# A hybrid encoder layer on one core: first loads of weight sums on POOL's queue, an own sum buffer in the last block, and separate columns for the final norm

## The chip, the core and the metric

The kernel runs on one core of one Trainium2 chip. The metric is the device time in microseconds. The engines are named as in the profile: PE is TensorE (PEld its weight loads), DVE VectorE, ACT ScalarE, POOL GpSimd, and SP SyncE, which here only issues transfers. Each of SP, ACT and POOL has a queue of transfers of its own; in the profile's queue names q1 is SP's, q10 ACT's and q0 POOL's ("software").

## The reference, cut to what matters

```python
x += 1/2 * SwiGLU_1(RMSNorm(x))          # 1024 -> 2816 -> 1024, 512 tokens
x += concat(ssd_out, attn_out) @ W_out   # a mixer between the two
x += 1/2 * SwiGLU_2(RMSNorm(x))
return rms_norm(x, final_norm)

def swiglu(h, w_gate, w_up, w_down):
    return (jax.nn.silu(h @ w_gate) * (h @ w_up)) @ w_down
```

All is float32. What follows touches the two feed-forward layers (FFN1, FFN2) and the final norm; the mixer is not changed.

## The kernel before

**Three matmuls for one.** Each float32 operand is split into a high part (a cast on ACT) and a low part (a subtraction on DVE); a product is then three matmuls. For a unit of weights the cast is line 272 and the subtraction line 274 (`usplit`); the results go to four pairs of `xw` tiles in turn.

**Units.** The 22 tiles of the hidden dimension are taken in 11 pairs, d = 0 to 10. In FFN1 d = 0 and 1, in FFN2 d = 0 are computed plainly in four units, A11, A21, A12, A22 (gate and up, each over half of the inner dimension: A12 and A22 need the second half of `x`). All others are computed with seven products of sums, P1 to P7, as in Strassen's scheme, and so are the down projections, in blocks of up to four d's; a piece c of a block is two d's. In the names below A[0] to A[3] are the four quarters of the weights of one d, W0 to W3 those of a piece of the down projection ("a0", "a10": its first d). A unit's weights are 512 KB in SBUF as 128 x 1024 floats; the last piece, a10, has half of that.

**Sums made by transfers.** P5 needs A[2]+A[3]; P6 adds A[0] to that, P3 adds A[1]. The sum stands in one of four half-buffers in the wide tiles s40 and s52: `first` (line 324) copies A[2] into it from SP's queue, `more` (line 327) adds the others by accumulating transfers, which only POOL issues. P7 adds a quarter onto the raw tile `g` of P1, also through POOL. Plain quarters are loaded raw by SP into four `raw` buffers (line 320).

**Order.** `program` lists the units in the order in which PE takes them. Weights are split three units ahead of their use (`Stream.get`), and each job's transfers are issued some units ahead, as its list of moves says (`(14, before, first)`: at most 14 units ahead and, once the job `before` has been split, which is when its buffer comes free). A scheduling layer sets the order on each engine from this.

**The last block.** The down projection of FFN2's last three d's (8, 9, 10) runs as ("S", 2, P, pieces): its first units take one piece at a time. P6 and P3 of piece a10 take the buffer in which P5's sum stood.

**The final norm.** `after2` runs when a 128-token tile t of one half o of `x` is complete: Square with a sum on ACT, a multiplication by the norm's weights on DVE, and, when both halves of a tile are there, the columns v, sqrt, reciprocal and one Newton step (`rq_*` tags, one buffer each), then the scalings and the transfers out.

Of the kernel before, what the change touches and what calls it, by code (L numbers as in the profile page):

```python
# [14 lines left out]
P = 128  # L15
# [22 lines left out]
def hybrid_block(ctx: ExitStack, tc, xT, xt, par, wgu1, wd1, ws1, win, wdt, wv, wo, rbt, wgu2, ws2, fin, out):  # L38
# [50 lines left out]
    class Job:  # L89
# [6 lines left out]
        def move(self, ahead, force=False):  # L96
            while self.moves and (force or ahead <= self.moves[0][0]):
                lead, after, fn = self.moves[0]
                if after == "raw":

                    after = ws.raws[-4] if len(ws.raws) > 3 else None
                    if not after or after.parts is not None:
                        ws.raws.append(self.holds)
                if after and after.parts is None:
                    assert not force
                    return
                fn()
                self.moves.pop(0)
# [172 lines left out]
    def program(plain, by_tokens):  # L281


        if plain == 1:
            out = [("A11", 0), ("A21", 0), ("A12", 0), ("P1", 1), ("P5", 1), ("A22", 0), ("P6", 1), ("P2", 1), ("P7", 1)]
        else:
            out = [(a, d) for d in range(plain) for a in ("A11", "A21", "A12", "A22")]
            out += [(p, plain) for p in ("P5", "P1", "P6", "P2", "P7")]
        out = [("P", p, d) for p, d in out]
        for d in range(plain + 1, ND):  # L290
            out += [("P", p, e) for p, e in (("P5", d), ("P1", d), ("P3", d - 1), ("P4", d - 1), ("P6", d), ("P2", d),
                                             ("P7", d))]
            for n in range(2):
                if d == BLOCKS[n][1]:
                    out += [("S", n, p, (0, 1)) for p in DOWN]
        last = [("P", p, ND - 1) for p in ("P3", "P4")]
        if by_tokens == 3:
            return out + last + [("S", 2, p, (c,)) for c in range(2) for p in ("P5", "P1") + ("P2",) * (c == 0)] + [
                ("S", 2, "P6", (0, 1)), ("S", 2, "P2", (1,))] + [("S", 2, p, (0, 1)) for p in ("P7", "P3", "P4")]
        out += [("D", 2, 0, 0)] + last + [("D", 2, 1, 0), ("D", 2, 0, 1), ("D", 2, 1, 1)]  # L300
        return out + [("D", 2, o, c) for o in range(2, KD) for c in range(2)]

    def ffn_weights(wgu, plain, by_tokens, wst, wd=None):


        bufs, jobs, views = {}, {}, []

        def view(d):
            if d not in bufs:
# [11 lines left out]
            return go  # L321

        def first(d, src):
            return lambda: nc.sync.dma_start(out=view(d), in_=src)

        def more(get, src):
            return lambda: G.dma_start(out=get(), in_=src, accum_op=ALU.add)  # L327
# [1 line left out]
        def product(p, d, A):  # L329

            sum_ = lambda: view(d)
            raw = {"P1": "g", "P2": "g2", "P4": "u2"}.get(p)
            if p[0] == "A":
                n = ("A11", "A12", "A21", "A22").index(p)
                j = Job(lambda: usplit(bufs[p, d]), (6, "raw", whole((p, d), A[n])))
            elif raw:
                j = Job(lambda: usplit(bufs[raw, d]), (6 if p == "P1" else 5, "raw",
                                                       whole((raw, d), A[("P1", "P2", "", "P4").index(p)])))
            elif p == "P5":
                views.append(d)  # L340
                before = jobs["P3", views[-5]] if len(views) > 4 else None
                j = Job(lambda: usplit(view(d)), (14, before, first(d, A[2])), (10, None, more(sum_, A[3])))
            elif p == "P6":
                j = Job(lambda: usplit(view(d)), (6, jobs["P5", d], more(sum_, A[0])))
            elif p == "P7":
                j = Job(lambda: usplit(bufs["g", d]), (6, jobs["P1", d], more(lambda: bufs["g", d], A[2])))
            else:
                j = Job(lambda: usplit(view(d)), (6, jobs["P6", d], more(sum_, A[1])))
            jobs[p, d] = j
            if p == "P7":  # L350
                jobs["P1", d].holds = j
            ws.jobs.append(j)
# [20 lines left out]
    class XCombos:  # L373
# [13 lines left out]
        def col(self, k):  # L387
            return pt[:, self.wcol + k:self.wcol + k + 1]
# [53 lines left out]
    def ffn(xc, n_plain, early, by_tokens, rc, between, after):  # L442
# [174 lines left out]
        for step in program(n_plain, by_tokens):  # L617
            if step[0] == "S":
                while later:
                    later.pop(0)()  # L620
                if step[1:3] == (2, "P6"):
                    next(between, None)
                down(*step[1:])
                past = step[1:3] == (1, DOWN[-1])
                continue
# [680 lines left out]
    fw = []  # L1306
    ssq = sb("rcol", [P, 2, NC])

    def after2(o, t):

        if (o, t) == (0, 0):

            S.activation(out=sb("rq_o0", [P, 1]), in_=ones[:, 0:1], func=AF.Sqrt)
        v = x[:, 4 * o:4 * o + 4, t * P:(t + 1) * P]
        sq = sb("fh", [P, SEQ], bufs=2)
        four = lambda t: t.rearrange("p (a b) -> p a b", a=4)
        S.activation(out=four(sq), in_=v, func=AF.Square, accum_out=ssq[:, o, t:t + 1])
        y[o, t] = slot(4 + 2 * t + o, None, F32)
        V.tensor_tensor(out=four(y[o, t]), in0=v, in1=four(fw[o]), op=ALU.mult)
        if o == t // 2 or t == 2:  # L1320
            return
        n = slice(2, 4) if t == 3 else slice(t, t + 1)
        N = [P, n.stop - n.start]
        v0 = sb("rq_o1", N)
        V.tensor_scalar(out=v0, in0=ssq[:, 1 - o, n], scalar1=1.0 / D, scalar2=EPS, op0=ALU.mult, op1=ALU.add)
        v = sb("rq_v", N)
        V.scalar_tensor_tensor(out=v, in0=ssq[:, o, n], scalar=1.0 / D, in1=v0, op0=ALU.mult, op1=ALU.add)
        sd = sb("rq_q", N)
        S.activation(out=sd, in_=v, func=AF.Sqrt)
        i = sb("rq_y", N)  # L1330
        V.reciprocal(out=i, in_=sd)
        q = sb("rq_t", N)
        V.tensor_tensor(out=q, in0=i, in1=i, op=ALU.mult)
        r = sb("rq_r", N)
        V.scalar_tensor_tensor(out=r, in0=q, scalar=-0.5, in1=v, op0=ALU.mult, op1=ALU.mult)
        rs = sb("rq_o0", N)
        V.scalar_tensor_tensor(out=rs, in0=r, scalar=1.5, in1=i, op0=ALU.add, op1=ALU.mult)
        for t in range(n.start, n.stop):
            for h in range(2):
                c = rs[:, t - n.start:t - n.start + 1]  # L1340
                if h == 0 or t > 1:
                    S.activation(out=y[h, t], in_=y[h, t], func=AF.Copy, scale=c)
                else:
                    V.tensor_scalar(out=y[h, t], in0=y[h, t], scalar1=c, scalar2=None, op0=ALU.mult)
                (nc.sync if h else S).dma_start(out=out[:, t, h * SEQ:(h + 1) * SEQ], in_=y[h, t])

    y = {}
    ffn(xc3, 1, early2, 3, rc, between2(), after2)


# [61 lines left out]
```

## Time and profile before

| what | value |
|---|---|
| runs | 1039.98, 1036.24, 1032.68 us; median 1036.24 us |
| profiled execution | 1034.42 us, span 1032.6 us |
| PE busy | 1007.5 us, 98% of the span |
| DVE, ACT, POOL busy | 809.0, 587.9, 162.2 us |
| mean granted TensorE clock | 0.995 |
| POOL's queue | 59.78 MB, 33.2% of the 16 DMA engines' span |
| SP's queue | 95.43 MB, 27.3% |

PE is busy nearly throughout, so the time before can only be shortened where PE waits, ahead of its first or behind its last matmul; it can be lengthened wherever something that PE needs comes later.

### The profile page before, as it was taken

How to read it: one execution, taken by the hardware profiler on the slowest of the kernel's cores; microseconds unless marked ns; L12 is line 12 of the kernel's file. 1: busy time of each engine (PE TensorE's matmuls, PEld its weight loads, DVE VectorE, ACT ScalarE, POOL GpSimd, SP SyncE). 2: the span in 40 equal slices, each digit the busy share in tenths (PEclk: the TensorE clock that was granted, in tenths of full speed). 3: DMA queues.
4: the chain of work that ended last, by engine and by line, in shares of the span. 5: the costliest groups of instructions: out<-in, count | busy, mean ns of one | idle time of the engine just before them, and what ended most of it. 6: DMA issues, size and time to landing. Idle time of an engine off the chain costs nothing.

```text
span 1032.6 us, 16130 instructions
## 1 busy us (share of the span) xinstructions
PE 1007.5 (98%) x6154; PEld 888.0 (86%) x6154; DVE 809.0 (78%) x1351; ACT 587.9 (57%) x929; POOL 162.2 (16%) x185
## 2 busy tenths in 40 slices
PE   9999999999999999999999999999999999999985
PEld 7899889998998777777878778879998899989974
DVE  7878767886676697978867999797687678867876
ACT  7556445653564456646656876656654356534535
POOL 1111112121120013323201011101212121212110
PEclk9999999999999999999999999999999999999998
DMA  9979888996753322222232223765888989989672
GB/s 317 291 156 236 181 231 185 227 205 160 195 117 97 102 82 62 66 78 68 67 100 74 82 83 103 227 140 124 193 201 188 236 198 229 202 194 206 154 143 81
DMA packets 47933, 162.14 MB, mean 157 GB/s; under 512 B 5232, under 2 KB 6000, under 8 KB 47856
## 3 DMA queue, kind: packets, MB, share of 16 engines
q0 software_dynamic: 16704, 59.78, 33.2%
q1 hardware_dynamic: 28272, 95.43, 27.3%
q10 hardware_dynamic: 2880, 5.91, 1.7%
q8 instruction: 48, 0.79, 0.3%
q14 instruction: 29, 0.24, 0.1%
HBM read 159.00 MB, written 2.10 MB: 156 GB/s over the span
## 4 chain that ended last, share of the span: by engine, by line
PE 80%; DVE 9%; issue 4%; DMA 4%; ACT 3%; POOL 0%; SPq 0%; ACTq 0%; DVEq 0%; POOLq 0%
PE mm L541 19%; PE aux L541 14%; PE mm L142 10%; PE mm L143 10%; PE mm L144 10%; PE aux L144 3%; PE aux L143 3%; PE aux L142 3%; DMA raw<-wgu 2%; DVE fs L829 2%; DMA s<-wgu 1%; DVE wlo L86 1%; DVE xw L274 1%; ACT xw L272 1%; PE aux L953 1%
## 5 line engine op out<-in xcount | busy, mean ns | idle before, releaser
L541 PE MATMUL mm<-s,xw 128*128 128x256 f32 x1824 | 229.2, 283 | 2.8 <-ACT fu L549 2.8
L541 PEld LDWEIGHTS mm<-s,xw 128*128 128x128 f32 x1824 | 222.2, 191 | 4.1 <-ACT fu L549 3.4
L272 ACT CAST xw<-raw 128x1024 fp32r<-128x1024 f32 (+1 forms) x127 | 131.3, 1036 | 150.1 <-PE mm L541 54.6
L274 DVE TENSOR_TENSOR xw<-raw,xw 128x1024 fp32r<-128x1024 f32 (+1 forms) x127 | 152.7, 1203 | 63.8 <-ACT xw L272 63.7
L541 PE MATMUL aux<-s,xw 128*128 128x256 f32 x1368 | 174.1, 283 | 0.0
L541 PEld LDWEIGHTS aux<-s,xw 128*128 128x128 f32 x1368 | 168.8, 192 | 0.6
L272 ACT CAST xw<-s 128x1024 fp32r<-128x1024 f32 (+1 forms) x87 | 90.0, 1035 | 118.7 <-PE mm L144 40.1
L142 PE MATMUL mm<-xw,whi 128*128 128x512 f32 x364 | 149.6, 411 | 0.0
L274 DVE TENSOR_TENSOR xw<-s,xw 128x1024 fp32r<-128x1024 f32 (+1 forms) x87 | 104.7, 1203 | 56.9 <-ACT xw L272 55.0
L143 PE MATMUL mm<-xw,whi 128*128 128x512 f32 x364 | 144.8, 398 | 0.0
L144 PE MATMUL mm<-xw,wlo 128*128 128x512 f32 x364 | 144.4, 397 | 0.0
L84 ACT CAST whi<-raw 128x512 fp32r<-128x512 f32 (+1 forms) x104 | 62.2, 601 | 66.1 <-PE mm L143 46.9
L327 POOL DMA_DIRECT2D s<-wgu x57 | 51.4, 940 | 307.7 <-DMA s<-wgu 139.7
L86 DVE TENSOR_TENSOR wlo<-raw,whi 128x512 fp32r<-128x512 f32 (+1 forms) x104 | 74.3, 715 | 13.9 <-ACT whi L84 13.4
L142 PEld LDWEIGHTS mm<-xw,whi 128*128 128x128 f32 x364 | 68.9, 189 | 16.5 <-issue 2.2
L143 PEld LDWEIGHTS mm<-xw,whi 128*128 128x128 f32 x364 | 68.8, 189 | 16.2 <-issue 1.2
L144 PEld LDWEIGHTS mm<-xw,wlo 128*128 128x128 f32 x364 | 68.7, 189 | 16.2
L327 POOL DMA_DIRECT2D s<-ws x30 | 26.1, 869 | 167.9 <-DVE xw L274 70.2
L143 PE MATMUL aux<-xw,s 128*128 128x512 f32 x106 | 42.1, 397 | 2.9 <-DVE xw L274 2.9
L144 PE MATMUL aux<-xw,s 128*128 128x512 f32 x106 | 42.2, 398 | 0.0
L142 PE MATMUL aux<-xw,s 128*128 128x512 f32 x106 | 41.6, 394 | 0.0
L884 POOL TENSOR_TENSOR fu<-dt,tri 128x512 fp32r<-128x512 f32 x16 | 18.9, 1189 | 95.9 <-PE aux L935 45.5
(297 smaller groups left out, 1745.8 us busy)
## 6 DMA issues: line engine op xcount, KB each, us to landing
raw<-wgu SPq DMA_DIRECT2D x68, 512.0 KB, 5.6
s<-wgu POOLq DMA_DIRECT2D x57, 512.0 KB, 6.2
raw<-win SPq DMA_DIRECT2D x28, 512.0 KB, 3.5
s<-ws POOLq DMA_DIRECT2D x27, 512.0 KB, 5.7
raw<-ws SPq DMA_DIRECT2D x27, 512.0 KB, 4.6
s<-wgu SPq DMA_DIRECT2D x19, 512.0 KB, 5.4
raw<-wgu POOLq DMA_DIRECT2D x19, 512.0 KB, 5.8
raw<-wo SPq DMA_DIRECT2D x12, 512.0 KB, 3.7
```

Of the source, the lines that this page charges most:

```text
L84: S.copy(out=hi, in_=src)
L86: V.tensor_tensor(out=lo, in0=src, in1=f(hi), op=ALU.subtract)
L142: T.matmul(ps, lhsT=sh, rhs=mh, start=start, stop=False, skip_group_check=skip)
L143: T.matmul(ps, lhsT=sh, rhs=ml, start=False, stop=False, skip_group_check=skip)
L144: T.matmul(ps, lhsT=sl, rhs=mh, start=False, stop=stop, skip_group_check=skip)
L272: S.copy(out=hi, in_=src)
L274: V.tensor_tensor(out=lo, in0=src, in1=f(hi), op=ALU.subtract)
L327: return lambda: G.dma_start(out=get(), in_=src, accum_op=ALU.add)
L541: T.matmul(ps[:, j * HS:(j + 1) * HS], lhsT=sw[:, j, k], rhs=m, start=(p in ("P1", "P2", "P5") and j == 0 and k == 0 and n == 0), stop=(k ...
L829: V.scalar_tensor_tensor(out=y[:, d:SEQ], in0=u[:, 0:SEQ - d], scalar=cw(j), in1=y[:, d:SEQ], op0=ALU.mult, op1=ALU.add)
L884: G.tensor_tensor(out=r, in0=f(src[:, c, h0:h0 + 4]).unsqueeze(2).broadcast_to([P, 4, P]), in1=tri.unsqueeze(1).broadcast_to([P, 4, P]), o ...
L953: T.matmul(py[HD * (h % 2):HD * (h % 2) + HD, (h // 2) * P:(h // 2 + 1) * P], lhsT=xd[:, h * HD:(h + 1) * HD], rhs=st["m"][h // 4][:, (h % ...
```

## The change

Four things are changed.

1. `first` goes to POOL's queue. In the steady part it is issued three units after the unit that frees its buffer, and the A[3] accumulation of P5 comes at most 8 units ahead instead of 10.
2. Piece a10 of FFN2 gets its own buffer for P6 and P3, `(2, 10, 2)`: W2, W3 and W0 are summed there afresh, and P3 adds W1 onto it.
3. In the last block P1 of piece a10 comes before P5, and the final norm's weights are asked for one step earlier.
4. The final norm's small columns get places of their own in a free tile; a dummy Sqrt behind the first Square loads the table early; one half of each output tile is scaled on ACT and the other on DVE; all eight output transfers go through SP.

```diff
@@ Job.move
+                elif type(after) is tuple:
+
+                    after, n = after
+                    if not force:
+                        after = ws.jobs[min(ws.jobs.index(after) + n, len(ws.jobs) - 1)]
@@ program
-            return out + last + [("S", 2, p, (c,)) for c in range(2) for p in ("P5", "P1") + ("P2",) * (c == 0)] + [
-                ("S", 2, "P6", (0, 1)), ("S", 2, "P2", (1,))] + [("S", 2, p, (0, 1)) for p in ("P7", "P3", "P4")]
+            return out + last + [("S", 2, p, (0,)) for p in ("P5", "P1", "P2")] + [
+                ("S", 2, p, (1,)) for p in ("P1", "P5")] + [("S", 2, "P6", (0, 1)), ("S", 2, "P2", (1,))] + [
+                ("S", 2, p, (0, 1)) for p in ("P7", "P3", "P4")]
@@ ffn_weights
         def first(d, src):
-            return lambda: nc.sync.dma_start(out=view(d), in_=src)
+            return lambda: G.dma_start(out=view(d), in_=src)
...
-                before = jobs["P3", views[-5]] if len(views) > 4 else None
-                j = Job(lambda: usplit(view(d)), (14, before, first(d, A[2])), (10, None, more(sum_, A[3])))
+                before = (jobs["P3", views[-5]], 3) if len(views) > 4 else None
+                j = Job(lambda: usplit(view(d)), (14, before, first(d, A[2])), (8, None, more(sum_, A[3])))
+            elif p == "P6" and d == LAST:
+
+                v = d + (2,)
+                views.append(v)
+                j = Job(lambda: usplit(view(v)), (16, (jobs["P3", views[-5]], 3), first(v, A[2])),
+                        (11, None, more(lambda: view(v), A[3])), (6, None, more(lambda: view(v), A[0])))
...
-                j = Job(lambda: usplit(view(d)), (6, jobs["P6", d], more(sum_, A[1])))
+                v = d + (2,) if d == LAST else d
+                j = Job(lambda: usplit(view(v)), (6, jobs["P6", d], more(lambda: view(v), A[1])))
@@ after2
-        if (o, t) == (0, 0):
-
-            S.activation(out=sb("rq_o0", [P, 1]), in_=ones[:, 0:1], func=AF.Sqrt)
...
         S.activation(out=four(sq), in_=v, func=AF.Square, accum_out=ssq[:, o, t:t + 1])
+        if (o, t) == (0, 0):
+
+            scr.append(slot(14, None, F32))
+            S.activation(out=scr[0][:, 100:101], in_=ssq[:, 0, 0:1], func=AF.Sqrt)
...
+        rs = norm(20 * t, n)
         for t in range(n.start, n.stop):
+            c = rs[:, t - n.start:t - n.start + 1]
+            S.activation(out=y[0, t], in_=y[0, t], func=AF.Copy, scale=c)
+            V.tensor_scalar(out=y[1, t], in0=y[1, t], scalar1=c, scalar2=None, op0=ALU.mult)
             for h in range(2):
-                c = rs[:, t - n.start:t - n.start + 1]
-                if h == 0 or t > 1:
-                    S.activation(out=y[h, t], in_=y[h, t], func=AF.Copy, scale=c)
-                else:
-                    V.tensor_scalar(out=y[h, t], in0=y[h, t], scalar1=c, scalar2=None, op0=ALU.mult)
-                (nc.sync if h else S).dma_start(out=out[:, t, h * SEQ:(h + 1) * SEQ], in_=y[h, t])
+                nc.sync.dma_start(out=out[:, t, h * SEQ:(h + 1) * SEQ], in_=y[h, t])
```

The new function `norm(c, n)` holds the column steps that stood in `after2`, each with a column of its own.

**POOL at the start of the program.** The two memsets are the constants; s40 and s52 hold the first four sums (d = 2, d = 3, d = 4 and piece a0). Before:

```order
L66 MEMSET ones_3_64 128x128
masks.py:197 MEMSET ident_4_66 128x128
masks.py:199 ISA
masks.py:199 AFFINE_SELECT ident_4_66<-ident_4_66 128x128 [waits Pool_49]
L327 DMA s40_45_150<-wgu1 128x1024 [waits DMAHW7_49]
L327 DMA s40_45_150<-wgu1 128x1024 [waits DMAHW0_49]
L327 DMA s52_113_472<-wgu1 128x1024 [waits DMAHW0_49]
L327 DMA s52_113_472<-ws1 128x1024 [waits DMAHW3_49]
```

After (line 331 is `first`, line 334 `more`):

```order
L66 MEMSET ones_3_64 128x128
masks.py:197 MEMSET ident_4_66 128x128
L331 DMA s40_45_150<-wgu1 128x1024
masks.py:199 ISA
masks.py:199 AFFINE_SELECT ident_4_66<-ident_4_66 128x128 [waits Pool_49]
L334 DMA s40_45_150<-wgu1 128x1024 [waits DMASW0_49]
L331 DMA s40_45_150<-wgu1 128x1024
L331 DMA s52_113_472<-wgu1 128x1024
L331 DMA s52_113_472<-ws1 128x1024
L334 DMA s40_45_150<-wgu1 128x1024 [waits DMASW2_49]
L334 DMA s52_113_472<-wgu1 128x1024 [waits DMASW3_49]
L334 DMA s52_113_472<-ws1 128x1024 [waits DMASW4_49]
```

The four first loads now stand on POOL with no wait of their own, ahead of or between the first accumulations, each of which waits for the landing of a transfer of the same queue.

**SP at the start.** `raw_92` is A[2] of d = 0 (A21's weights), `raw_95` A[1] (A12's), `raw_144` A[3] (A22's); `x` is the input. Before:

```order
L320 DMA raw_9_92<-wgu1 128x1024 [waits DMAHW0_49]
L669 DMA x_2_62<-xT 128x1024 [waits DMAHW1_49]
L320 DMA raw_10_95<-wgu1 128x1024 [waits DMAHW2_49]
L671 DMA x_2_62<-xT 128x1024 [waits DMAHW3_49]
L320 DMA raw_42_144<-wgu1 128x1024 [waits DMAHW4_49]
L320 DMA raw_43_146<-wgu1 128x1024 [waits DMAHW6_49,DMAHW5_49,DVE_49]
L320 DMA raw_44_148<-wgu1 128x1024 [waits DMAHW0_49,DVE_49]
L324 DMA s40_45_150<-wgu1 128x1024 [waits DMAHW7_49]
L324 DMA s40_45_150<-wgu1 128x1024
L320 DMA raw_50_192<-wgu1 128x1024 [waits DMAHW2_49,DMAHW1_49,DVE_49]
```

The rows up to `raw_148` stand in the same order after the change, with line 320 become 327; the two rows of line 324 are gone from SP, and `raw_192` follows at once.

**POOL in the last block.** `s40` from `ws2` with 128x512 is the new sum of piece a10, `s40` from `wgu2` are the sums of d = 10, `raw` from `wgu2` is P7's sum of d = 10. After:

```order
L334 DMA s40_1356_6797<-wgu2 128x1024 [waits DMASW6_49,DVE_49]
L334 DMA raw_1771_9757<-wgu2 128x1024 [waits DMAHW4_49,DMAHW2_49,DMAHW6_49,DMASW1_49,DVE_49]
L331 DMA s40_1356_6797<-ws2 128x512 [waits DMASW7_49,DMASW2_49,DVE_49]
L334 DMA s40_1356_6797<-ws2 128x512 [waits DMASW2_49]
L334 DMA s40_1356_6797<-ws2 128x512 [waits DMASW4_49,DMASW3_49]
L334 DMA s40_1356_6797<-wgu2 128x1024 [waits DMASW0_49,DVE_49]
L334 DMA s52_1422_7110<-ws2 128x1024 [waits DVE_49]
L334 DMA raw_1812_10079<-ws2 128x1024 [waits DMAHW3_49,DMAHW6_49,DMAHW0_49,DVE_49]
```

Before the change the A[1] accumulation of d = 10 (P3's sum) followed the raw one directly:

```order
L327 DMA raw_1771_9757<-wgu2 128x1024 [waits DMAHW6_49,DMAHW0_49,DVE_49]
L327 DMA s40_1356_6797<-wgu2 128x1024 [waits DMASW5_49,DMASW3_49,DVE_49]
L327 DMA s52_1422_7110<-ws2 128x1024 [waits DMASW6_49,DVE_49]
L327 DMA raw_1812_10079<-ws2 128x1024 [waits DMAHW2_49,DMAHW3_49,DMAHW0_49,DVE_49]
L327 DMA s52_1422_7110<-ws2 128x512 [waits DMASW0_49,DVE_49,Activation_49]
```

So three transfers of piece a10, each waiting for the one before, came between P7's sum and P3's sum of d = 10; the accumulation of W0 onto P5's buffer (the 128x512 row of `s52` with a wait on ACT) is gone from behind them.

## Rows read from the trace of the kernel before

**Rows 1.** The page, part 1: busy time, share, instructions of each engine.

```profile
PE 1007.5 (98%) x6154; PEld 888.0 (86%) x6154; DVE 809.0 (78%) x1351; ACT 587.9 (57%) x929; POOL 162.2 (16%) x185
```

**Rows 2.** PE's waits, the two largest: total us, times, longest.

```profile
PE aux L143 <- DVE xw L274: 2.9, 1, 2.9
PE mm L541 <- ACT fu L549: 2.8, 2, 2.1
```

**Rows 3.** Transfers from 8 to 20 us: queue, packets, MB, share of 16 engines.

```profile
q1 hardware_dynamic: 1390, 4.91, 102.2%
```

**Rows 4.** Line 320 at 7.62 us, the load of A[3], d = 0: issue and landing.

```profile
L320 SPq DMA_DIRECT2D raw<-wgu x1: 562/562/562, 7.6 to 7.6; - x1
...
DMA to landing us min/median/max: 8.2/8.2/8.2
```

**Rows 5.** Timeline, 19 to 25 us: start, duration, engine, line, [idle before].

```profile
19.13 1.22 DVE L274 TENSOR_TENSOR xw<-raw,xw 128x1024 fp32r<-128x1024 f32 x1
...
20.00 1.01 POOL L327 DMA_DIRECT2D s<-wgu  x1 [18.49 <-DMA s<-wgu]
...
24.80 0.49 PE L142 MATMUL aux<-s,xw 128*128 128x512 f32 x1
```

**Rows 6.** Transfers from 20 to 36 us: queue, packets, MB, share.

```profile
q1 hardware_dynamic: 605, 2.20, 38.3%
q0 software_dynamic: 288, 1.05, 33.6%
q10 hardware_dynamic: 471, 1.74, 28.1%
```

**Rows 7.** Chain of waits, 815 to 842 us (FFN2): start, us, what.

```profile
818.07 0.86 POOL raw L327
...
827.74 6.62 DMA s<-wgu
...
834.46 0.31 ACT xw L272
...
838.43 3.13 PE mm L541 x24
```

**Rows 8.** Timeline of POOL at the same place.

```profile
827.74 1.78 POOL L327 DMA_DIRECT2D s<-wgu  x2 [8.81 <-DMA s<-wgu]
```

**Rows 9.** Line 327's transfer issued at 818.07 us: time to landing.

```profile
DMA to landing us min/median/max: 8.3/8.3/8.3
```

**Rows 10.** Timeline of DVE, POOL, ACT and PE, 959 to 979 us.

```profile
959.08 1.23 DVE L274 TENSOR_TENSOR xw<-s,xw 128x1024 fp32r<-128x1024 f32 x1
...
966.46 0.88 POOL L327 DMA_DIRECT2D s<-wgu  x1 [7.67 <-DVE xw L274]
...
972.34 1.05 ACT L272 CAST xw<-s 128x1024 fp32r<-128x1024 f32 x1 [0.67 <-PE mm L541]
...
977.97 1.24 PE L541 MATMUL mm<-s,xw 128*128 128x256 f32 x9
```

**Rows 11.** Timeline of POOL, ACT and PE, 995 to 1002 us.

```profile
995.25 0.87 POOL L327 DMA_DIRECT2D s<-ws  x1 [10.70 <-issue]
...
999.34 0.62 ACT L272 CAST xw<-s 128x512 fp32r<-128x512 f32 x1 [1.96 <-DMA s<-ws]
...
1001.33 0.50 PE L143 MATMUL aux<-xw,s 128*128 128x512 f32 x1 [2.85 <-DVE xw L274]
```

**Rows 12.** Chain of waits, 990 to 1033 us: start, us, what.

```profile
995.25 4.06 DMA s<-ws
...
1003.01 0.43 PE mm L142
...
1006.40 0.23 PE mm L143
```

**Rows 13.** Timeline of ACT and DVE, 1018 us to the end.

```profile
1020.40 1.28 ACT L1329 ACT_TABLE_LOAD   x1
...
1025.75 0.16 DVE L1331 RECIPROCAL rq_y<-rq_q 128x1 f32<-128x1 f32 x1 [2.46 <-ACT rq_q L1329]
...
1028.16 0.72 ACT L1342 ACTIVATE s<-s,rq_o 128x512 f32<-128x512 f32 x1 [0.81 <-DVE rq_o L1337]
```

More of the change, by code (lines that the diff above doesn't have):

```diff
@@ L306, in ffn_weights @@
         bufs, jobs, views = {}, {}, []
+        LAST = (2, ND - 1)
         def view(d):
@@ L620, in ffn @@
                     later.pop(0)()
-                if step[1:3] == (2, "P6"):
+                if step[1:] == (2, "P5", (1,)):
                     next(between, None)
@@ L1307, in hybrid_block, with norm @@
     ssq = sb("rcol", [P, 2, NC])
+    def norm(c, n):
+        N = n.stop - n.start
+        t = iter(range(c, c + 8 * N, N))
+        col = lambda: scr[0][:, (i := next(t)):i + N]
+        v0, v, sd, i, q, r, rs = [col() for _ in range(7)]
+        V.tensor_scalar(out=v0, in0=ssq[:, 0, n], scalar1=1.0 / D, scalar2=EPS, op0=ALU.mult, op1=ALU.add)
+        V.scalar_tensor_tensor(out=v, in0=ssq[:, 1, n], scalar=1.0 / D, in1=v0, op0=ALU.mult, op1=ALU.add)
+        S.activation(out=sd, in_=v, func=AF.Sqrt)
+        V.reciprocal(out=i, in_=sd)
+        V.tensor_tensor(out=q, in0=i, in1=i, op=ALU.mult)
+        V.scalar_tensor_tensor(out=r, in0=q, scalar=-0.5, in1=v, op0=ALU.mult, op1=ALU.mult)
+        V.scalar_tensor_tensor(out=rs, in0=r, scalar=1.5, in1=i, op0=ALU.add, op1=ALU.mult)
+        return rs
     def after2(o, t):
-        if (o, t) == (0, 0):
-            S.activation(out=sb("rq_o0", [P, 1]), in_=ones[:, 0:1], func=AF.Sqrt)
         v = x[:, 4 * o:4 * o + 4, t * P:(t + 1) * P]
@@ L1317, in after2 @@
         S.activation(out=four(sq), in_=v, func=AF.Square, accum_out=ssq[:, o, t:t + 1])
+        if (o, t) == (0, 0):
+            scr.append(slot(14, None, F32))
+            S.activation(out=scr[0][:, 100:101], in_=ssq[:, 0, 0:1], func=AF.Sqrt)
         y[o, t] = slot(4 + 2 * t + o, None, F32)
         V.tensor_tensor(out=four(y[o, t]), in0=v, in1=four(fw[o]), op=ALU.mult)
-        if o == t // 2 or t == 2:
+        if (1 - o, t) not in y or t == 2:
             return
         n = slice(2, 4) if t == 3 else slice(t, t + 1)
[L1323 to L1337, printed above, removed]
+        rs = norm(20 * t, n)
         for t in range(n.start, n.stop):
+            c = rs[:, t - n.start:t - n.start + 1]
+            S.activation(out=y[0, t], in_=y[0, t], func=AF.Copy, scale=c)
+            V.tensor_scalar(out=y[1, t], in0=y[1, t], scalar1=c, scalar2=None, op0=ALU.mult)
             for h in range(2):
-                c = rs[:, t - n.start:t - n.start + 1]
-                if h == 0 or t > 1:
-                    S.activation(out=y[h, t], in_=y[h, t], func=AF.Copy, scale=c)
-                else:
-                    V.tensor_scalar(out=y[h, t], in0=y[h, t], scalar1=c, scalar2=None, op0=ALU.mult)
-                (nc.sync if h else S).dma_start(out=out[:, t, h * SEQ:(h + 1) * SEQ], in_=y[h, t])
-    y = {}
+                nc.sync.dma_start(out=out[:, t, h * SEQ:(h + 1) * SEQ], in_=y[h, t])
+    y, scr = {}, []
     ffn(xc3, 1, early2, 3, rc, between2(), after2)
```

## The prediction

> **What bounds the kernel now.** I read the page's busy times first: PE is busy 98% of the span [rows 1], so the other engines and the transfers count only where PE waits for them, before its first unit and behind its last. PE's own waits come next. The two largest are one of 2.9 us for DVE in the last block and two, 2.8 us together, for ACT's copy in front of P7 [rows 2]. The chains of waits in front of these show that a transfer of POOL's is behind each [rows 7, 11]. So a gain of this change is bounded by these 5.7 us, what slow matmuls behind one of them add, and the tail behind the last matmul. A loss has no such bound: at the start of the program PE takes each unit soon after its weights are there, and whatever delays them moves everything behind.
>
> **Part 1a: first loads on POOL, at the start.** This is the largest term, and no copy by POOL's queue stands in the trace before; all that POOL moved there are accumulations. Before, POOL issued nothing until 20.00 us, because its first accumulation waited for a first load that SP had put behind all the loads of the first plain units [rows 5]. From 8 to 20 us the transfer engines were full with one queue, SP's: 4.91 MB in 12 us, 102% [rows 3], or 1.27 us for a load of 512 KB (0.524 MB / 4.91 MB x 12 us = 1.28). In this order the last load that d = 0 needs, A22's, was issued at 7.6 and landed 8.2 later, at 15.9 us [rows 4]; its low part began at 19.13 and took 1.22, PE began A22 at 24.80 [rows 5].
>
> After the change POOL issues the first load of d = 2 right behind its memsets, beside SP's first loads; then the accumulation on it as soon as it has landed, then at once the first loads of d = 3, d = 4 and a0, then their accumulations, each when its copy has landed. Together that is four copies and four accumulations of 512 KB that now meet SP's loads. The price of an accumulation comes from the stretch from 20 to 36 us, where two of them ran beside SP's and ACT's queues: 33.6% of 16 us for 1.05 MB [rows 6], 2.7 us for one. Four copies are 4 x 1.27 = 5.1 us, four accumulations 10.8 us.
>
> How much of the 15.9 us gets in front of A22's load depends on how the queues share the engines. If POOL's and SP's queues take turns one for one, then of SP's seven halves of a megabyte still open at 6 us the last lands only when seven of POOL's have gone too. Then all eight are ahead: A22's load lands at 15.9 + 15.9 = 31.8 us. Behind a late landing the cast (1.05, [rows 10]) and the low part (1.22) come, with some 0.2 of handing over, so A22 starts at 34.3 instead of 24.80: +9.5. If the accumulations get less than their turn, as the 1.05 MB against 2.20 and 1.74 in that stretch suggest [rows 6], about one of them stays behind A22's load: 2.7 less, +6.8. I take the middle, **+8**. As ends I keep +4 (copies and two accumulations ahead: 10.5 us, landing at 26.4, A22 at 28.9) and +14 (all eight ahead, and three stalls each with the slow matmuls of the next part but one, 3 x 1.6 on top of 9.5). PE is busy from there to the end, so nothing takes this back.
>
> The Trainium skill ("DMA: Bandwidth & Descriptors", section "SWDGE vs HWDGE vs iDMA") has a rule that speaks against this part: plain copies belong on SP's or ACT's queue, accumulations on GpSimd's; it goes with a somewhat later first byte on GpSimd's side ("Advanced Engine Details and Errata", "DGE: Hardware vs Software": about 1 us against about 600 ns). No run here shows that difference for a copy; by that figure alone each first load would be 0.4 us later (an estimate from that page), 0.8 us for the two places of the next part, and the sum 0.8 higher. The section "Queues, rings and completion order" of the first page says that a transfer engine goes round the queues packet by packet; by that rule alone the start would cost the 9.5 of one-for-one turns, and the sum would be 1.5 higher. The trace agrees that queues share, and has POOL's below its turn.
>
> **Part 1b: first loads in the steady part.** There a late first load costs only where the buffer came free late: P5 of d = 6, in both FFNs. In FFN2 the chain reads: accumulation issued 827.74, landed 6.62 later; the cast of P5's sum at 834.46 stands on ACT in front of the copy that PE waits for, and PE goes on at 838.43, 3.97 after that cast began [rows 7]. The accumulation was waiting for the first load [rows 8]. Moved to POOL, that first load stands in one queue behind P7's accumulation onto the raw tile, issued at 818.07 and 8.3 under way, until 826.4 [rows 7, 9]. Where before the two shared the engines, now the one waits for the other. That costs nothing where nobody else is moving data, and up to one accumulation's 2.7 us where SP's loads fill the gap. I take half, 1.3, and twice, since FFN1 has the same chain (2.1 us of the 2.8 in [rows 2]): **+2.6**, ends 0 and +5. Taking first loads off SP frees SP's raw loads, but no raw load ends a wait of PE there [rows 2], so no gain stands against it. POOL itself is 16% busy [rows 1]; 31 more issues of some 0.9 us beside it cost nothing.
>
> **Part 2: the last block.** The 2.85 us stall at 998.5 to 1001.33 comes from W0's accumulation onto the buffer of P5 of a10: issued at 995.25, 4.06 under way, cast at 999.34, low part, PE [rows 11, 12]. With a buffer of its own that sum is made some units earlier; the stall goes. After it PE ran its matmuls at 0.43 us each, later at 0.23 [rows 12]. The slow ones go from 1001.33 to about 1005, eight of them: 8 x 0.20 = 1.6 us. Together **-4.4**; what is late next is DVE's low parts in the same place, for which I keep 0.5 back in the range. The reordered P1 and P5 of a10 have the same matmuls and cost nothing.
>
> The price is paid ahead of it. Three transfers of 256 KB, each waiting for the one before, now stand in POOL's order before P3's accumulation for d = 10, which was issued at 966.46 and cast at 972.34 [rows 10]. The first can only begin when P3 of d = 9 has been split (low part 959.08 + 1.23 = 960.3, [rows 10]); with 4.06 for each [rows 12] and P7's accumulation ahead, they land at about 964.8 and 968.9, and the third and then P3's are issued by 969.9: 3.4 us later than before. From that cast to PE's next need, P7 of d = 10 at 977.97 [rows 10], there are 5.6 us, of which the work on ACT takes the same 3.97 as in d = 6; 1.7 us are slack. Remains **+1.7** (0 to +2.5).
>
> **Part 3: the tail.** Before, a table load of 1.28 us on ACT stands in front of the sqrt of the last tiles; a scaling on ACT holds the next sqrt, for which DVE waits 2.46 us; the last scaling begins at 1028.16 [rows 13]. The load moves to the first Square, and the columns no longer wait for one another, so up to 3.7 us could go. Against it all eight transfers out are issued by SP one after another, where ACT took four before. I take about half, **-1.7**, ends -3 and 0. The early dummy's load in the mixer goes as well, beside work.
>
> **The sum.** 8 + 2.6 - 4.4 + 1.7 - 1.7 = +6.2 us against the profiled execution's 1034.42: 1040.6. The median of the runs is 1036.24, 1.8 us above that execution, and by it the sum would be 1042.4. I forecast between them, 1041.5.
>
> **The rivals.**
> Rival A, faster than before: the start costs nothing. SP's loads were issued within the first 8 us, and POOL has to make each transfer in its own program; if its copies are served only where SP's queue leaves gaps, A22 starts at 24.80 as before. For it speaks POOL's low share in [rows 6]; against it that SP's queue left no gap [rows 3] and that accumulations made it late as soon as they ran. Then 1034.4 - 4.4 - 1.7 + 1.7 + 0 to 2.6 gives 1030 to 1032.6. It decides if A22 starts before some 27 us. Chance 0.12.
>
> Rival B, slower by over 1%: one-for-one turns, and slow matmuls behind each wait. If PE waits in front of each of A21, A12 and A22 and takes up each at the pace of 0.43 [rows 12], the start costs up to 14 us and the time is 1046.6 or more, to 1050. For it speaks that both other queues there ran slower the moment accumulations began; against it POOL's share. It decides if A22 starts later than 37 us. Chance 0.30.
>
> Rival C, the change doesn't do what it says: the own buffer's three transfers come so late that its sum is no earlier than W0's before, the stall of 2.85 stays, or the wait only moves to DVE. Then 4.4 comes back: 1045. Against it: by the reckoning above they land around 973, twenty us ahead. Chance 0.08.
>
> My forecast, 1036 to 1046, has 0.50. **How the numbers follow.** About 1% (10.4 us) is what a measurement of this kernel can tell from no change. Forecast, A and C lie within it: 0.63 with some loss at the edges; B makes most of the 0.33 for slower; faster would need a gain of over 10 us, and stalls and tail hold 5.7 + 1.6 + 3.7 = 11 at the very most: 0.04. The range from 1030 to 1050 takes in A's lower end and B's upper.
>
> **What would show it.** In the profile after: PE's waits at the start for the casts and low parts of A12 and A22, A22 starting at 31 to 35 us, SP's loads landing up to 16 us later and POOL's queue moving 4 MB by 36 us; the waits in front of P7 of d = 6 near 2.0 and 3.4 instead of 0.7 and 2.1; a wait of 1 to 2 us at P7 of d = 10; no wait of 2.9 in the last block; the last scaling some 2 us nearer to the last matmul. I am wrong if A22 starts near 25 us, or if a stall appears that the trace before has nothing of, such as PE waiting for sums whose A[3] now comes two units later.

## The result, and the profile after

The changed kernel took 1048.14 us (median of 4 runs, 1046.24 to 1048.78) against 1034.46 us for the kernel before: ratio 1.0124, 95% interval 1.0075 to 1.0172. It is slower by 13.7 us. A second set of runs gave 1050.70 us and 1.0150 (1.0106 to 1.0193). The sign is as forecast. The time lies inside the full range, 1030 to 1050 us, but above the 1036 to 1046 us that had half of the chance; the forecast sum of +6.2 us was less than half of the loss by these medians, and about half of the 11.9 us by which the span of the profile grew.

The page of the changed kernel, its first lines (answers to [rows 1]):

```profile
span 1044.5 us, 16102 instructions
...
PE 1012.7 (97%) x6154; PEld 893.3 (86%) x6154; DVE 808.6 (77%) x1353; ACT 586.2 (56%) x926; POOL 179.4 (17%) x216
```

The span grew by 11.9 us and PE's busy time by only 5.2. The rest is waiting. PE's waits (answers to [rows 2]):

```profile
PE mm L555 <- ACT fu L563: 10.8, 3, 7.1
PE mm L147 <- ACT xw L696: 3.1, 1, 3.1
...
PE aux L210 <- DVE s L203: 1.3, 2, 0.6
```

The wait of 2.9 us for DVE in the last block is gone. In its place stand one of 7.1 us for ACT's copy, a longer one in front of the very first matmul (line 696 splits its weights; 1.4 us before) and a small one at the norm's columns.

To find where the loss arises I took PE's first matmul of several units in each trace and subtracted the same unit's time before. A step between two columns is what was lost or won there. F1 and F2 are the two FFNs; "P3 d6" lies behind the waits at d = 6, "P3 d10" behind P7 of d = 10 (the waits that the prediction and this text name by d = 6 stand in front of P7 of d = 5: the cast of P5's sum of d = 6 comes before its copy on ACT), "P4 a10" is the last unit, "end" the span. All kernels run for this study are in the table; they are told of below.

```
us later than before, by one profile of each kernel
kernel       P5 d2 F1  P3 d6 F1  P5 d2 F2  P3 d6 F2  P6 d10  P3 d10  P4 a10    end
changed           4.0       5.2       5.2       7.9     7.9    16.7    12.6   11.9
again             8.3       8.7       8.9      13.0    15.2    23.5    19.2   18.6
start_pool        7.0       5.3       5.7       4.7     8.6     8.6     8.9    8.8
start_one         3.6       1.3       1.5       2.1     2.1     2.1     2.8    2.9
start_sp          0.6       2.0       2.5       5.1     5.1    11.5     7.2    6.4
first_sp         -0.1      -0.0      -0.5      -1.4     0.6     8.8     4.4    3.4
no_own            5.9       8.0       8.1       9.1     9.1     9.1     9.6    9.0
late_own          8.5      11.0      10.8      15.4    19.3    19.3    15.1   14.4
held              0.5       9.7       9.4      12.2    12.2    21.9    17.7   17.1
norm_only         0.1      -2.2      -3.0      -3.9    -3.9    -3.9    -2.4   -3.6
best             -0.1      -1.1      -1.5      -1.4    -1.4    -1.4    -5.8   -6.7
```

The changed kernel, read along its row: 4.0 at the start, 1.2 and 2.7 at d = 6 of the two FFNs, 8.8 at P7 of d = 10, -4.1 in the last block, -0.7 from the last unit on. The sum is 11.9. (Counted from the end of the last matmul, the tail is 11.3 instead of 11.7 us, 0.4 shorter, and the last block 4.4; inside the last unit the order of matmuls differs.)

**The start.** Timeline of POOL and PE in the changed kernel (answers to [rows 5]):

```profile
1.40 0.70 POOL L331 DMA_DIRECT2D s<-wgu  x1 [0.25 <-issue]
...
9.09 0.88 POOL L334 DMA_DIRECT2D s<-wgu  x1 [6.59 <-DMA s<-wgu]
...
8.82 0.80 PE L147 MATMUL mm<-s,xw 128*128 128x512 f32 x1 [3.12 <-ACT xw L696]
9.41 0.63 PE L148 MATMUL mm<-s,xw 128*128 128x512 f32 x1
...
13.81 0.40 PE L147 MATMUL mm<-s,xw 128*128 128x512 f32 x1
...
28.25 0.49 PE L147 MATMUL aux<-s,xw 128*128 128x512 f32 x1
```

POOL issues the copy of d = 2 at 1.40 us, 0.15 us behind SP's load of the first half-tile that A11 needs. That half-tile now takes 6.9 us to land, not 4.9. These are the answers for it in the changed kernel:

```profile
L680 SPq DMA_DIRECT2D raw<-wgu x1: 653/653/653, 1.2 to 1.2; - x1
...
DMA to landing us min/median/max: 6.9/6.9/6.9
```

and in the kernel before, with PE's first row there:

```profile
L666 SPq DMA_DIRECT2D raw<-wgu x1: 653/653/653, 1.2 to 1.2; - x1
...
DMA to landing us min/median/max: 4.9/4.9/4.9
...
6.87 0.50 PE L142 MATMUL mm<-s,xw 128*128 128x512 f32 x1 [1.39 <-ACT xw L682]
```

In the profiles without a copy of POOL's there, this load took 3.6 to 4.9 us, in the six with it 6.5 to 7.2. So PE begins at 8.82 instead of 6.87. After its 3.1 us of idleness the first matmuls then come every 0.43 us, up to 13.25, where later ones come every 0.23. A21 begins 3.7 us late, and A22 at 28.25 still 3.45 late: no wait for A22's weights is in PE's list.

**The last block.** Timeline of POOL and ACT, and PE's row at P7 of d = 10 (answers to [rows 10]):

```profile
968.61 0.57 POOL L331 DMA_DIRECT2D s<-ws  x1 [1.85 <-DVE xw L279]
973.03 0.85 POOL L334 DMA_DIRECT2D s<-ws  x1 [3.85 <-DMA s<-ws]
978.34 0.86 POOL L334 DMA_DIRECT2D s<-ws  x1 [4.46 <-DMA s<-ws]
978.94 1.14 POOL L334 DMA_DIRECT2D s<-wgu  x1
...
989.19 1.04 ACT L277 CAST xw<-s 128x1024 fp32r<-128x1024 f32 x1 [9.57 <-DMA s<-wgu]
...
993.15 1.22 PE L555 MATMUL mm<-s,xw 128*128 128x256 f32 x4 [7.07 <-ACT fu L563]
```

The three transfers of a10 wait for one another, and P3's sum of d = 10 is issued behind them at 978.94. Everything there runs 7.95 us later than before, so 966.46 would be 974.4: the issue is 4.5 us late. It then takes 10.15 us to land, as the chain of waits shows, against 5.5 before (966.46 to the cast at 972.34, less 0.35 of ACT's own):

```profile
978.94 10.15 DMA s<-wgu
...
989.19 0.16 ACT xw L277
```

It shares POOL's queue with W0 of a10, issued 0.6 us ahead of it, and the engines with a load of SP's issued at 980.1. Late issue and late landing are 9.1 us; some of it was slack, 7.1 us are PE's wait, and behind the wait PE runs slowly again. The table by stretch, 986 to 1000 us (columns: window, length, busy times with counts, granted clock, DMA share, GB/s):

```profile
986.00:993.00 7.00, 0.08 (x1) 0.00 (x0) 2.73 (x6) 3.81 (x7) 0.00 (x0) 0.76 0.07 16
993.00:997.70 4.70, 4.55 (x25) 4.55 (x26) 4.70 (x7) 1.57 (x3) 0.63 (x1) 0.63 0.18 56
997.70:1000.00 2.30, 2.30 (x14) 1.72 (x13) 1.36 (x3) 2.06 (x3) 0.23 (x1) 1.00 0.60 71
```

The granted clock of 0.63 over 4.7 us is a mix of its two levels (1.2 and 2.4 GHz); the 24 matmuls of P7 took 4.58 us where they take 3.1 at full clock [rows 7].

### The profile page after: what moved, and what is told of

Read it like the earlier page. It is cut to its first block, busy times and chain, and to the rows that moved or that the text cites. A ratio compares the mean times of both kernels' runs of the same rounds, so it can differ in the third digit from the quotient of the medians.

```text
span 1044.5 us, 16102 instructions
## 1 busy us (share of the span) xinstructions
PE 1012.7 (97%) x6154; PEld 893.3 (86%) x6154; DVE 808.6 (77%) x1353; ACT 586.2 (56%) x926; POOL 179.4 (17%) x216
## 4 chain that ended last, share of the span: by engine, by line
PE 74%; DVE 12%; DMA 5%; issue 4%; ACT 3%; POOL 0%; SPq 0%; ACTq 0%; DVEq 0%; POOLq 0%
PE mm L555 18%; PE aux L555 13%; PE mm L147 10%; PE mm L149 10%; PE mm L148 10%; PE aux L147 3%; PE aux L149 3%; PE aux L148 3%; DVE xw L279 2%; DMA s<-wgu 2%; DMA raw<-wgu 2%; DVE fs L843 2%; DVE wlo L86 1%; PE aux L1203 1%; ACT xw L277 1%
## 5 line engine op out<-in xcount | busy, mean ns | idle before, releaser
L555 PE MATMUL mm<-s,xw 128*128 128x256 f32 x1824 | 233.5, 286 | 10.8 <-ACT fu L563 10.8
L555 PEld LDWEIGHTS mm<-s,xw 128*128 128x128 f32 x1824 | 226.2, 194 | 12.5 <-ACT fu L563 11.6
L148 PEld LDWEIGHTS mm<-xw,whi 128*128 128x128 f32 x364 | 68.5, 188 | 16.3 <-issue 1.2
```

Of the source, the lines that this page charges most:

```text
L148: T.matmul(ps, lhsT=sh, rhs=ml, start=False, stop=False, skip_group_check=skip)
L555: T.matmul(ps[:, j * HS:(j + 1) * HS], lhsT=sw[:, j, k], rhs=m, start=(p in ("P1", "P2", "P5") and j == 0 and k == 0 and n == 0), stop=(k ...
```

## The experiments

**start_sp.** The first four first loads back on SP (in each FFN; those of FFN2 run beside the mixer's end).

```diff
-            return lambda: G.dma_start(out=view(d), in_=src)
+            return lambda: (nc.sync if views.index(d) < 4 else G).dma_start(out=view(d), in_=src)
```

> The changed kernel with only the first four first loads (d = 2, 3, 4 and a0 of FFN1) back on SP's queue; all others stay on POOL's. Theory: these four cost 4.0 us at the start and nothing else. A22 starts at 24.8 instead of 28.25 and the span is 1040.5 instead of 1044.5; the wait of 7.1 us at P7 of d = 10 stays. Rival: the delay at the start comes from SP's own loads being asked for in another order, or is given back later anyway; then A22 stays near 28 or the span near 1044.

Ratio 1.0093 (1.0068 to 1.0118), span 1039.0. The loss at the start fell from 4.0 to 0.6 us, as the theory had it, and the loss at P7 of d = 10 stayed, though smaller (6.4 us instead of 8.8):

```profile
PE mm L555 <- ACT fu L563: 7.3, 3, 3.6
```

The start's loss is these four transfers, and it isn't given back later.

**start_pool.** The same from the other side: the kernel before, with only FFN1's first four on POOL.

```diff
-            return lambda: nc.sync.dma_start(out=view(d), in_=src)
+            return lambda: (G if wd is not None and views.index(d) < 4 else nc.sync).dma_start(out=view(d), in_=src)
```

> The kernel before with only the first four first loads of FFN1 (d = 2, 3, 4 and a0) on POOL's queue. Theory: the loss at the start stands alone, 4 to 8.5 us by what the three profiles with that start showed (A21, at the end of A11(1) at the latest, 4.0, 5.9 and 8.5 us late), and nothing else changes: span 1036.5 to 1041. Rival: the loss at the start is a matter of the run, not of these four transfers, since it differed between profiles: then the span is within 1.5 us of 1032.6.

Ratio 1.0089 (1.0057 to 1.0121), span 1041.4: 9 us slower with only these four transfers moved, a little over the theory's upper end. The rival is out. 7.0 us are lost by P5 of d = 2; the changes behind it (down to 4.7, then 8.6) stand in stages whose code is the same as before. Single waits at d = 6 and d = 9 differ that much between profiles; whether a later start helps to make them is not shown.

**start_one.** The kernel before, with only the very first of them on POOL (`views.index(d) < 1` in the same line).

> The kernel before with only the very first of the first loads (d = 2 of FFN1) on POOL's queue; its accumulation then follows at about 8 us. Theory: the loss at the start goes with the bytes that are put ahead; one copy and one accumulation of the eight leave PE's first unit 2 us late (raw half-tile landing near 8 instead of 6.2 us) and no second wait at 42 us: 1.5 to 3 us lost by P5 of d = 2, span 1034 to 1035.5. Rival: the loss is made by the accumulations of d = 3, 4 and a0 that run beside A1 of d = 1; then under 1 us is lost.

Ratio 1.0036 (1.0017 to 1.0055), span 1035.5. PE's first row is the changed kernel's to 0.01 us, and the second wait is absent:

```profile
8.81 0.80 PE L142 MATMUL mm<-s,xw 128*128 128x512 f32 x1 [3.12 <-ACT xw L682]
...
PE aux L205 <- DVE s L198: 0.2, 1, 0.2
```

3.6 us were lost by P5 of d = 2, more than the theory's 1.5 to 3. One copy costs nearly as much as four do in the changed kernel's profile: this part of the loss doesn't go with the bytes ahead, it is PE's late begin (1.95 us) and the slow matmuls behind it (nine at 0.43 instead of 0.23, 1.8 us). What the other three add is a second wait, and its size changes from run to run.

**again.** The changed kernel once more.

> The changed kernel once more, for how far one profile of it speaks for others. Theory: the loss at the start lies again between 4 and 8.5 us, with a second wait at 40 to 43 us that follows the landing of A1 of d = 1; the wait at P7 of d = 10 is again 6 us or more; the ratio is 1.010 to 1.016. Rival: the wait at P7 of d = 10 was of that one run; then it is under 3 us.

Ratio 1.0150, span 1051.2; the wait at P7 of d = 10 was 6.6 us, so it belongs to the kernel and not to one run. The loss at the start was 8.3 us. The second wait is PE's at the norm's columns:

```profile
42.80 0.50 PE L210 MATMUL aux<-s,onesr 128*128 128x512 f32 x1 [3.23 <-DVE s L203]
```

and the chain of waits behind it, from 20 us on:

```profile
20.31 12.44 DMA raw<-wgu
...
33.91 1.23 DVE xw L279
...
39.28 1.23 DVE xw L279
...
42.14 0.61 DVE s L203
```

A transfer of SP's, A[1] of d = 1, took 12.4 us to land beside POOL's copies and accumulations (4.9 before). DVE takes its work in order: the low part of that unit stands in front of the columns of the first norm, though PE needs the unit itself only later. With a landing of 10.9 us in the changed kernel's first profile PE waited 0.6 there, with 12.4 to 13.1 in the others between 3.2 and 4.1. In all five profiles with these four copies PE's row at the columns comes 10.04 or 10.05 us behind the landing of that load, at whatever time it landed (30.03 to 32.98 us), so this landing sets the second wait. Why it came 2 to 3 us earlier in the first profile isn't settled.

**first_sp.** All first loads on SP, the rest of the change as it is.

```diff
-            return lambda: G.dma_start(out=view(d), in_=src)
+            return lambda: nc.sync.dma_start(out=view(d), in_=src)
```

> The changed kernel with all first loads back on SP's queue; own sum buffer, block order and final norm stay. Theory: the start and the wait at P7 of d = 6 of FFN2 go back to before (4.0 and 1.3 us, and the slow matmuls behind), but the wait at P7 of d = 10 stays at 5 us or more, since W3 and W0 of a10 still stand in front of P3's accumulation on POOL: span about 1037. Rival: it is the first loads in POOL's queue that make P3's sum of d = 10 late; then that wait falls under 1.5 us and the span is about 1030.

Ratio 1.0047 (1.0027 to 1.0068), span 1036.0. The start and d = 6 are back at the times before or better, and PE's wait at P7 of d = 10 stays at 6.6 us:

```profile
PE mm L555 <- ACT fu L563: 10.6, 3, 6.6
```

The rival is out: that wait is made by the accumulations of a10 that stand in front, from whatever queue its first load comes. (The other two of the three stand at d = 6 of FFN1 and at P7 of d = 9.)

**no_own.** The changed kernel without the own buffer: the branch `elif p == "P6" and d == LAST` taken out, and P3 back to `view(d)`.

> The changed kernel without the own sum buffer of piece a10: P6 and P3 take P5's buffer as before, all first loads stay on POOL. Theory: the wait of 7.1 us at P7 of d = 10 and the 1.5 us of slow matmuls behind it go, the old wait in the last block (2.9 us and 1.6 us of slow matmuls) comes back: span about 1040. Rival: the wait at P7 of d = 10 is made by first loads and accumulations in one queue and stays above 3 us: span 1044 or more.

Ratio 1.0147 (1.0106 to 1.0188), span 1041.6. By P3 of d = 10 nothing is lost against P6 of d = 10 (9.1 and 9.1), so the wait there is gone, as the theory had it. The old wait of the last block is back, at another unit, since P1 and P5 have changed places:

```profile
PE mm L147 <- ACT xw L277: 3.1, 1, 3.1
```

The span fell by 2.9 us and not by 4.5, because this run lost 5.9 us at the start. Its runs lie from 1043 to 1053 us; the times alone would not have told the two apart, the places of the waits do.

**late_own.** The own buffer put where d = 10's sum stood (one view later in the turn of the four), so that the data themselves hold its three transfers back until P3 of d = 10 is split.

```diff
-                views.append(v)
+                views.extend([None, v])
```

> The changed kernel with the own sum buffer of a10 put where d = 10's sum stood, not where d = 9's stood, so that its three transfers come behind P3's accumulation of d = 10 on POOL. Theory: the wait at P7 of d = 10 is gone or under 0.5 us and the old wait in the last block does not come back: span about 1036 (1044.5 less 8.8). Rival: the own sum is then too late for P6 of a10, and a wait of 2 us or more appears there: span 1038 or more.

POOL's timeline: P3's sum of d = 10 is issued at once, at 966.46 + 19.29, the delay of everything there, and a10 follows 9 us later:

```profile
985.75 0.87 POOL L334 DMA_DIRECT2D s<-wgu  x1 [7.83 <-DVE xw L279]
994.80 0.57 POOL L331 DMA_DIRECT2D s<-ws  x1 [8.18 <-DVE fh L502]
```

Nothing is lost at P7 of d = 10 (19.3 and 19.3), and the old wait does not come back (-4.2 by P4 of a10): both as the theory had it. The span it gave, 1036, was missed by 11 us, since this run lost 8.5 at the start, 7.1 at the two d = 6 and 3.9 at P7 of d = 9. The median, 1043.64 us, ratio 1.0095 (1.0068 to 1.0122), is lower than the changed kernel's in either set of runs, though the intervals of the ratios overlap.

**held.** The first four copies on POOL, but behind A22's load: one column of its raw tile is copied into each sum buffer first.

```diff
...
+                    G.tensor_copy(out=flat[0][:, 0:1], in_=flat[1][:, 0:1])
...
                 G.dma_start(out=view(d), in_=src)
```

> The changed kernel, all first loads on POOL, but those first four wait until A22's load has landed (by a one-column copy on POOL from A22's raw tile into each sum buffer, which the load then overwrites). Theory: not the queue but the bytes ahead of SP's loads cost time; A22 starts within 1 us of 24.80 and the loss at the start is under 1.5 us, the rest of the loss stays: span about 1041. Rival: copies by POOL's queue slow the start whenever they run; then A11 of d = 1 starts late and 3 us or more stay lost by P5 of d = 2.

Ratio 1.0152, span 1049.7. Only the first half came: 0.5 us lost by P5 of d = 2. Then PE waited 4.5 us for a sum's cast at P6 of d = 2 and more behind it, some 9 us by P3 of d = 6. Neither theory had that. POOL's timeline shows one reason:

```profile
16.27 8.55 POOL L335 COPY s<-raw 128x1 f32<-128x1 f32 x4 [14.75 <-DMA raw<-wgu]
24.76 1.98 POOL L336 DMA_DIRECT2D s<-wgu  x3
```

The four one-column copies took 8.55 us beside a DVE that was busy throughout, so the loads went out at 24.8 and not at 16.3, and each accumulation behind them later than before: the first at 34.14 instead of 20.00 [rows 5]. So this kernel shows that A22 is on time when the copies come later, and does not show what POOL's queue would do with copies at 16 us. The Trainium skill ("SBUF — State Buffer", "SBUF: two separate sides") says that a DVE instruction with two SBUF inputs and a GpSimd instruction that reads SBUF lock each other out of a shared port pair for the whole instruction. The 2.1 us of a one-column copy would fit such a lock, but no run here separates it from other causes.

**norm_only.** The kernel before with the new final norm alone.

> The kernel before with the new final norm alone (columns, table load behind the first Square, scalings, SP's eight transfers out). Theory: the tail from the last matmul to the end is 0.7 us shorter, nothing else changes: span about 1031.9, the same within what can be told. Rival: the table load, now in the middle of the last block, delays a cast and PE by up to its 1.28 us, and the tail's gain is lost: span 1032.6 or more.

Ratio 1.0009 (0.9987 to 1.0032): no difference that can be told. From the last unit to the end the profile won 1.2 us, and PE lost 1.5 us in the last block (-3.9 and -2.4 in the table): the rival came beside the theory. ACT's and PE's rows there:

```profile
1004.90 1.28 ACT L1333 ACT_TABLE_LOAD   x1
...
1006.30 0.60 ACT L272 CAST xw<-raw 128x512 fp32r<-128x512 f32 x1
...
1006.96 0.73 PE L142 MATMUL mm<-xw,s 128*128 128x512 f32 x2 [1.20 <-ACT xw L272]
```

The table load, taken out of the tail, now holds up a cast that PE waits for 1.2 us. In the changed kernel and in best, with the new block order, no wait of PE follows the same load. The 3.9 us that this profile gained ahead of it are at d = 6 of both FFNs and between them, in unchanged code.

**best.** What the others leave: first loads on SP under the rules of before, the own buffer in the later place, the new block order and norm.

```diff
-            return lambda: G.dma_start(out=view(d), in_=src)
+            return lambda: nc.sync.dma_start(out=view(d), in_=src)
-                before = (jobs["P3", views[-5]], 3) if len(views) > 4 else None
-                j = Job(lambda: usplit(view(d)), (14, before, first(d, A[2])), (8, None, more(sum_, A[3])))
+                before = (jobs["P3", views[-5]], 0) if len(views) > 4 else None
+                j = Job(lambda: usplit(view(d)), (14, before, first(d, A[2])), (10, None, more(sum_, A[3])))
-                views.append(v)
+                views.extend([None, v])
```

> The changed kernel with all first loads on SP, issued and followed up as before (14 and 10 units ahead, no units past the release), the own sum buffer of a10 where d = 10's sum stood, the new block order and the new norm. Theory: the old wait in the last block with its slow matmuls is gone (4.4 us) and the tail is 0.7 us shorter, with no new wait: span about 1027.5, ratio 0.995. Rival: DVE's low parts hold PE in the last block instead, or P3's sum of d = 10 is late again; then span 1031 or more.

1030.13 us against 1033.69, ratio 0.9952 (0.9930 to 0.9973): faster than both kernels, with the ratio that the theory gave (the span, 1025.9, is below the 1027.5 of the theory, but 1.4 us of that arose at d = 6 in unchanged code). Between P3 of d = 10 and P4 of a10 it wins 4.4 us, in the tail 0.9. Its waits for ACT's copy are the two in front of P7 at d = 6, as before:

```profile
PE mm L555 <- ACT fu L563: 1.9, 2, 1.1
```

## Why the prediction was right and wrong, by its steps

**Bound and sign: right.** A gain was bounded by two waits and the tail, and transfers ahead of the first units had no such bound. Slower it was. The time lies in rival B's band (1046.6 to 1050), but B was to show by A22 starting later than 37 us, and A22 started at 28.25: B's time came without its sign; slow matmuls behind waits did come, but at other places. That the range held is in part luck. The start lost 4.0 us less than forecast in this profile, and that hid more than half of the 7.1 us by which the price in part 2 was too small.

**Part 1a, the start: size within its ends, place wrong.** The step by which A22's load lands at 31.8 us and A22 starts at 34.3 failed. A22's load landed at about 22 (its cast ran at 22.1), and PE waited for neither A12 nor A22. From 9 to 13.4 us POOL's queue moved almost nothing (the first two rows: packets, MB, share of 16 engines). From 13.4 to 22.1 us the two queues did take turns one for one, by their bytes, but POOL had fewer transfers to take them with:

```profile
q1 hardware_dynamic: 577, 1.79, 101.3%
q0 software_dynamic: 10, 0.04, 4.6%
...
q0 software_dynamic: 418, 1.54, 57.4%
q1 hardware_dynamic: 433, 1.58, 45.6%
```

Each accumulation waits for its copy: the first was issued at 9.09 us, the other three at 21.34, 23.90 and 26.52, too late to stand ahead of A22's load, where the forecast had put all eight transfers, or all but one. (The 1.05 MB of [rows 6], read there as less than a turn, were the only two accumulations that POOL had issued in that stretch.) I had looked only at the last load of d = 0 and at the sum of bytes ahead of it. The loss came at two places that I did not cost: the very first half-tile, 2 us late behind one single copy (start_one shows it alone, start_sp without it), with slow matmuls on top; and a load of d = 1 that PE did not need yet but behind which DVE had queued the norm's columns (again, start_pool). Measured 4.0 to 8.5 us in five profiles of the same start, against 8 with ends 4 and 14.

**Part 1b, d = 6: the wait was mis-sized, the slow matmuls were missing.** 1.2 and 2.7 us measured, 1.3 each forecast. In FFN2 the wait grew from 0.7 to 2.0 us, the 1.3 forecast. In FFN1 it shrank from 2.06 to 1.75; what was lost there is a slower clock behind it (last section). Since norm_only and best differ from before by 1 to 2 us at the same place, with its code unchanged, these two terms are not known better than that from single profiles. By the times, start_sp and first_sp, which differ only in the first loads behind the first four of each FFN, stand at 1038.38 us with them on SP and 1042.17 with them on POOL: 3.8 us for all of these loads together (what they do to P7 of d = 10 included), against the 2.6 forecast for d = 6.

**Part 2, the gain: right.** -4.4 forecast, -4.1 measured (-4.4 to the end of the last matmul), and late_own, first_sp and best repeat it (-4.2, -4.4, -4.4, from P3 of d = 10 to P4 of a10).

**Part 2, the price: the term that failed.** "Remains +1.7 (0 to +2.5)" was 8.8. The chain of three transfers, each waiting for the one before, was reckoned well (issue 3.4 us later forecast, 4.5 measured). But I let the accumulation behind it land in the time that it took before the change. It was now one of two in POOL's queue, with a load of SP's beside: 4.6 us more. And a wait of 7 us has slow matmuls behind it, 1.5 us. That these transfers are the cause is shown from both sides: first_sp keeps them and keeps the wait, no_own takes them away and late_own moves them behind, and the wait is gone. How the 9.1 us divide between late issue and late landing is read from the trace and was not tried apart.

**Part 3, the tail: smaller.** -0.7 measured from the last unit on, -0.4 from the end of the last matmul (-1.2 and -1.1 in norm_only, -0.9 and -0.7 in best), -1.7 forecast. Scalings end 5.1 us behind the last matmul (1033.2) instead of 8.0, a gain of 2.9, but SP's eight transfers, one after another, are now what ends last, as was feared:

```profile
1035.69 2.65 ACT L1356 ACTIVATE s<-s,s 128x512 f32<-128x512 f32 x4
...
1037.61 0.49 DVE L1357 TENSOR_SCALAR s<-s,s 128x512 f32<-128x512 f32 x1
...
1036.16 4.47 SPq L1359 DMA_DIRECT2D outT<-s  x8
```

Scalings end at 1038.3, SP's issues at 1040.6. The load that left the tail I had costed at nothing: no wait of PE follows it in the changed kernel, but with the old block order it was not free where it went (norm_only).

**Rivals A and C** did not happen: the start cost time in every run that had the four copies there, and the own buffer did remove the wait it was meant for.

## What to carry to other kernels

An instruction without a wait is issued as early as its engine can (POOL's first copy at 1.40 us): a rule of "so many units ahead" in the program's planning didn't hold POOL's first copies back, only data did. Before moving loads to an idle queue, ask what lands at the same time on the other queues, beginning with the first byte that the bound engine waits for, and what else is queued in order behind each delayed load. And a chain of dependent transfers put ahead of another on the same queue cost it twice here, once at its issue and once in landing; placing a buffer where its data come free later can be the whole remedy.

## What the runs showed of the hardware that was not expected

Waits of nearly the same length on PE had different sequels. At P7 of d = 5, in front of which P5 of d = 6 is cast in FFN1, PE waited 2.06 us before the change and then ran its 24 matmuls in 3.14 us, with a granted clock of 1.00. In the changed kernel it waited 1.75 us and took 4.62 us, with 0.63 over that stretch (1.2 GHz for a part of it). Before:

```profile
166.44 3.14 PE L541 MATMUL mm<-s,xw 128*128 128x256 f32 x24 [2.06 <-ACT fu L549]
...
166.40:170.00 3.60, 3.56 (x29) 3.56 (x30) 3.60 (x6) 2.02 (x3) 0.86 (x1) 1.00 1.01 160
```

After, with the row of FFN2 below it:

```profile
170.12 4.62 PE L555 MATMUL mm<-s,xw 128*128 128x256 f32 x24 [1.75 <-ACT fu L563]
...
844.90 4.38 PE L555 MATMUL mm<-s,xw 128*128 128x256 f32 x24 [2.00 <-ACT fu L563]
...
170.00:174.60 4.60, 4.48 (x25) 4.48 (x26) 4.60 (x7) 1.65 (x3) 1.41 (x2) 0.63 0.98 154
```

So a wait of about 2 us can cost 1.5 us more than its length, and whether it does can't be read from the length alone. A longer one shows the same: at the norm's columns PE waited 3.23 us in again, and from 44.40 us on its matmuls came every 0.43 us; in no_own it waited 3.38 us at the same place, and the pace stayed at 0.23:

```profile
41.95 0.50 PE L210 MATMUL aux<-s,onesr 128*128 128x512 f32 x1 [3.38 <-DVE s L203]
...
45.03 0.39 PE L149 MATMUL aux<-s,xw 128*128 128x512 f32 x1
```

At the start the matmuls from 8.82 to 13.25 us ran at the slow pace while the granted clock of that stretch reads 1.00 (third column from the end); there only the spacing of the matmuls shows it:

```profile
8.00:11.00 3.00, 2.18 (x5) 1.81 (x6) 1.93 (x3) 2.61 (x5) 1.91 (x4) 1.00 1.06 411
```
